# Two low-rank norms in a transformer block: row sums by transposing products and a small root, or sums over all partitions at once and a root on 128x512

## The chip, the cores and the metric

The kernel runs on one core of a Trainium2 chip. The metric is device time in microseconds (us) of one execution, the median of several. Each engine takes its own instructions in order and waits on semaphores: TensorE (PE; its weight loads are listed as PEld), VectorE (DVE), ScalarE (ACT), GpSimd (POOL) and SyncE (SP), which issues most of the transfers.

## What is computed

One block on 512 tokens of width 1024: a projection of the normalised input, a gated linear attention (GLA, 4 heads), a latent attention (MLA, 8 heads), a merge, and a squared-ReLU MLP. The change concerns the two latents of the MLA branch: `cq` (384 features) and `ckv` (256 features) are normalised per token before they are multiplied up to queries, keys and values.

```python
def rmsnorm(x, g):
    xf = x.astype(jnp.float32)
    y = xf * lax.rsqrt(jnp.mean(xf * xf, axis=-1, keepdims=True) + EPS)
    return (y * g.astype(jnp.float32)).astype(x.dtype)
...
    n = rmsnorm(h, g_mix[l])
    proj = n @ w_in[l]
    (gq, gk, gv, gr, z_gf, z_gb, cq, ckv, kr, z_ma, z_mb) = jnp.split(proj, SPLIT_IDX, axis=-1)
...
    q = (rmsnorm(cq, g_q) @ w_uq).reshape(B, S, H, MLA_QK_HEAD)
    kv = (rmsnorm(ckv, g_kv) @ w_ukv).reshape(B, S, H, MLA_NOPE + MLA_V)
```

## The kernel before

Precision is kept by splitting each fp32 operand into a rounded half and a rest (`split`: ACT writes the rounded half, DVE the rest); a product is then three PE passes (`mm3`: half by half, half by rest, rest by half). A projection of 128 columns (`proj_run`) is 24 matmuls of 512 columns. The input's own norm is applied afterwards: `R` (128x512) holds each token's factor on every partition, `r_x` (128x4) the same factors with tokens on partitions.

The latents are kept transposed, features on partitions and tokens along the row. `Latent.keep` stores a 128-feature piece with its gain (`cqc0` to `cqc2`, `ckvc0`, `ckvc1`) and its squares; `add_squares` adds those up into one 128x512 tile (`cqs2`, `ckvs1`). What is left to sum is over partitions, and this is done in four steps:

- `sums` (with `feature_sums`): four fp32 matmuls per latent, whose weights are 128 tokens of the squares and whose moving operand is one column of ones. Their result (`cqss`, `ckvss`) is 128x4, tokens on partitions. Two small DVE operations make it a mean, and POOL takes the power -1/2 on 128x4 (`cqr`, `ckvr`).
- `diagonals`: DVE multiplies by `r_x`, splits the 128x4 result and writes two 128x512 tiles of diagonal blocks (`cqdg`, `ckvdg`).
- `spread`: two matmuls of 512 columns with the matrix of ones bring every token's factor to every partition (`cqrs`, `ckvrs`, in PSUM).
- `normed`: DVE multiplies the kept pieces by that, ACT writes rounded halves (`cqhl0` to `cqhl2`, `ckvhl0`, `ckvhl1`), DVE the rests.

The work around it: for each GLA head h, `gla_scores` (tiles `bd`, `sc0`, `sc1`, `kt`), the gates of head h+1 (tile `l`, by ACT's exponential and logarithm, sums by DVE scans), `gla_state` (`gla2st`), `gla_out` (`gla2o`, `gla3o`), the squares and the root of the head's output (`gla2ss`, on ACT and POOL), and `gla_turn`, transposes of a finished head (`y12` to `y15`). Projections of the merge gate (`zb4` to `zb7`) and of queries and keys (`gq3`, `gk3`) lie between. For head 3 come the products that use the normalised latents: `ro0`, `ro1` (rotary part of the queries, from `cqhl` and the weights `wr0`, `wr1`, whose rests POOL computes), `uq0`, `uk0`, `uv0x`.

The order on each engine is fixed. Up to the end of the loop over heads 0 to 2 it is the order of the code; from there on, instructions are held back and issued by a long list of names (`SEQUENCE`), one queue letter and tile for each (`P` PE, `A` ACT, `D` DVE, `G` POOL, `S` SP). Stages of weights share rings of few buffers, so a transfer waits for the last reader of the buffer that it takes. PSUM has two rings of four banks ("at" and "mm"). At the very end, 20 matmuls of 64 columns into an unused tile (`tail`) run on PE behind the last product, while the last rows are scaled and stored.

Of the kernel before, what the change touches and what calls it, by code (L numbers as in the profile page):

```python
# [97 lines left out]
def tile_block(ctx: ExitStack, tc: tile.TileContext, t, out: bass.AP):  # L98
# [198 lines left out]
    def feature_sums(sq, name, tag="at"):
        tot = ps(tag, f"{name}ss")
        for j in range(NT):
            nc.tensor.matmul(tot[:, j : j + 1], sq[:, j * P : (j + 1) * P], ones[:, 0:1], start=True, stop=True)  # L300
        return tot
# [1707 lines left out]
    for x in range(2):  # L2009
# [4 lines left out]
        S:wr1f P:ckvss*4 D:ckvr D:cqc1 P:kt*4 S:wr1f D:ckvr P:y15*4 A:cqhl1 G:ckvr A:bds P:sc1*5 A:cqhl2 D:sc0 P:y14*4
        D:zb4 A:wr0h A:wk0h D:ckvr D:cqhl2 G:wr0l A:wk0h A:qF D:sc1*2 D:cqhl0 A:sc1 S:wk1f D:ckvrh D:ckvdg D:krsin
        D:ckvrl D:ckvdg D:cqhl1 D:sc1 P:zb5*24 A:wr1h D:sc0 A:yg4 D:zb5 G:wr1l A:cos D:kswap A:yg5 G:wk0l S:wq0f
        P:ro0*9 A:kT D:kr P:ckvrs*2 S:wq0f A:wk1h A:wk0h G:wk1l S:wq0f A:sc0 D:roa1 G:qF A:wk0h D:roa0 D:kr P:ro1*9
        G:wk0l D:ckvc0 D:ckvc1 A:ckvhl0 D:ckvhl0 D:kT A:tb5 D:rob1 A:wk1h D:rob0 A:kbuf0 D:roa0 A:ckvhl1 D:kbuf0
        A:wq0h P:zb6*24 A:ro0 D:sc0 G:wq0l D:ro0 G:wk1l S:zb7f P:gla3st*12 A:gla3s D:ckvhl1 G:wk0l P:gla3o1*12 D:roa1
        G:wk0l D:gla3s A:ro1 P:gla3o0*12 D:zb6 S:wq1f D:ro1 S:wq1f S:kbuf1 P:uq0*9 S:q001 S:q000 P:gla3o0*6 A:gla3sq  # L2020
        S:wq1f A:wk1h P:gla3o1*6 A:zb7h S:q000 G:wk1l S:q001 A:gla3sq P:uk0*6 D:zb7l A:gla3sq S:q211 A:q000 S:q110
        A:kbuf0 S:wq2f P:uv01*12 A:kbuf1 D:kbuf0 S:q110 A:gla3sq A:v01 G:gla3ss S:kbuf2 G:gla3ss A:wq1h S:q011 A:wk1h
        G:gla3ss A:q010 G:wq1l S:q010 D:grc D:grb S:q010 D:kbuf1 S:wq2f D:q011 S:w2_10 D:q001 S:wk2f D:grb D:v01
        S:q011 P:zb7*24 D:zb7 S:q211 P:s00*3 D:grc S:q210 P:s01*3 S:w2_20 D:top01 S:w2_30 D:top00 S:wq2f A:e00 P:uq1*9
        A:tb4 P:y17*4 A:q100 P:y16*4 A:e01 P:s03*3 S:q110 D:top03 A:wk2h S:q111 P:s11*3 A:yg6 G:wk2l D:tot00 D:e01
        S:kbuf3 A:e00 G:wk1l D:top11 A:e03 S:q111 P:uk1*6 D:q101 S:bo11f A:kbuf2 P:s02*3 A:wq2h S:q111 A:e11 P:s10*3
        G:wq2l S:bo11f D:top10 S:w2_20 D:top02 A:e10 A:e02 P:uv11*12 P:tp000*4 P:tp001*4 A:wk2h D:tot02 D:kbuf2
        A:pT000 G:wk2l D:tot10 A:tb6 S:kbuf3 D:pT010 P:uv10*12 S:w2_00 A:v10 P:s12*3 A:e02 S:q100 D:top12 A:pT001
        S:q100 D:e03 A:bo11h S:wk3f D:v10 P:uv00*12 S:q101 A:yg7 P:s13*3 P:uq2 D:top13 A:v00 S:kbuf2 A:e10 D:e11
        S:q101 D:pT011 A:e13 D:v00 A:e12 P:uq2*8 D:bo11l A:wk2h P:s31*3 G:wk2l A:tb7 P:tp010*4 P:tp011*4 A:pT000  # L2030
        D:top31 S:wq3f A:wk3h P:tp100*4 D:pT010 A:q200 S:wq3f A:e31 D:q201 D:tot12 P:uk2*6 D:e13 A:kbuf0 P:tp101*4
        S:q301 A:pT001 P:s21*3 S:h3 A:wk2h D:pT011 A:e12 G:wk2l D:top21 A:pT101 S:bo10f A:pT100 D:pT111 S:bo10f A:e21
# [15 lines left out]
        A:e50 P:s71*3 A:ghyo0 D:e61 G:w2_21 D:top71 A:e63 P:av4*4 G:w2_20 D:bo50l A:e71 P:s70*3 P:tp500*4 A:pT500
        D:tot62 P:tp510*4 S:w2_00 A:v30 D:top70 P:tp600*4 S:h2 A:gao1 D:e63 A:pT500 S:h0 D:pT510 G:gao1 A:pT600 S:h1
        D:v30 P:av4*7 D:pT510 G:yo1 P:wox0*3 D:tb4 P:tp501*4 G:zo0 A:pT501 P:wox1*3 G:glyo0 A:e70 D:pT511 P:s72*3  # L2050
        P:av5 D:pT610 P:tp511*4 G:my2 D:top72 A:pT501 P:s73*3 D:tot70 G:mx2 A:ghyo1 D:pT511 P:av5*2 A:e62 G:zo2 D:e71
# [149 lines left out]
```

## Time and profile before

| | |
|---|---|
| median of 3 runs | 732.03 us (731.73 to 732.14) |
| the profiled execution: its own time | 732.09 us |
| its span, first to last instruction | 730.3 us |
| around the span | 1.79 us |
| granted TensorE clock | 0.999 |
| busy: PE, DVE, ACT, POOL | 726.3, 619.8, 498.7, 225.8 us |

The page gives each engine's busy time and share of the span, the chain of work that ended last, and groups of instructions. The timeline gives start and duration of single instructions (neighbours merged, with their number), and in brackets how long the engine had been idle and for whom it waited. A line L90 or L76 is that of a recording helper, so instructions are told by their tiles.

### The profile page before, as it was taken

How to read it: one execution, taken by the hardware profiler on the slowest of the kernel's cores; microseconds unless marked ns; L12 is line 12 of the kernel's file. 1: busy time of each engine (PE TensorE's matmuls, PEld its weight loads, DVE VectorE, ACT ScalarE, POOL GpSimd, SP SyncE). 2: the span in 40 equal slices, each digit the busy share in tenths (PEclk: the TensorE clock that was granted, in tenths of full speed). 3: DMA queues.
4: the chain of work that ended last, by engine and by line, in shares of the span. 5: the costliest groups of instructions: out<-in, count | busy, mean ns of one | idle time of the engine just before them, and what ended most of it. 6: DMA issues, size and time to landing. Idle time of an engine off the chain costs nothing.

```text
span 730.3 us, 11455 instructions
## 1 busy us (share of the span) xinstructions
PE 726.3 (99%) x4174; PEld 641.2 (88%) x4174; DVE 619.8 (85%) x859; ACT 498.7 (68%) x846; POOL 225.8 (31%) x290
## 2 busy tenths in 40 slices
PE   9999999999999999999999999999999999999998
PEld 8888888888888888888888999889988998899987
DVE  6677887889988897789999789998699869987797
ACT  7456565595696864988866889545774477646976
POOL 1842020243843843226763512200111012100224
PEclk9999999999999999999999999999999999999999
DMA  9968683521222324657957899871987088814864
GB/s 323 346 176 198 210 180 88 84 62 29 58 58 59 89 46 110 184 158 189 251 88 208 196 205 201 187 215 57 245 182 201 9 223 206 206 59 134 183 89 143
DMA packets 82777, 112.06 MB, mean 153 GB/s; under 512 B 16384, under 2 KB 35712, under 8 KB 82720
## 3 DMA queue, kind: packets, MB, share of 16 engines
q1 hardware_dynamic: 65344, 77.81, 34.0%
q0 software_dynamic: 17088, 33.30, 27.3%
q8 instruction: 33, 0.54, 0.3%
q10 hardware_dynamic: 288, 0.22, 0.1%
q14 instruction: 24, 0.20, 0.1%
HBM read 106.32 MB, written 2.10 MB: 148 GB/s over the span
## 4 chain that ended last, share of the span: by engine, by line
PE 99%; issue 0%
PE f3x L90 3%; PE f2x L90 3%; PE f1x L90 3%; PE f0x L90 3%; PE first L90 3%; PE s L76 3%; PE av L76 3%; PE wox L76 3%; PE g2x L90 3%; PE g1x L90 3%; PE g0x L90 3%; PE gvx L90 3%; PE zax L90 3%; PE grx L90 3%; PE gk L90 2%; PE cq L90 2%
## 5 line engine op out<-in xcount | busy, mean ns | idle before, releaser
L90 POOL DMA_DIRECT2D w<-in_w_ff x32 | 38.6, 1205 | 240.1 <-DMA w<-in_w_ff 134.8
L76 ACT ACTIVATE e<-s,top 128x512 f32<-128x512 f32 x32 | 21.9, 688 | 8.5 <-DVE top L76 7.4
L76 DVE TENSOR_REDUCE top<-s 128x1 f32<-128x512 f32 x32 | 21.6, 682 | 5.8 <-PE s L76 5.6
L76 PE MATMUL s<-kbuf,q 96*128 96x512 f32 x96 | 26.3, 400 | 0.0
L76 PE MATMUL av<-pT,v 128*128 128x512 f32 (+1 forms) x108 | 25.2, 371 | 0.0
L76 DVE TENSOR_TENSOR pT<-tp,pT 128x512 fp32r<-128x512 f32 x32 | 21.7, 683 | 2.4 <-ACT pT L76 1.0
L76 ACT ACTIVATE pT<-tp 128x512 fp32r<-128x512 f32 x32 | 18.5, 596 | 6.1 <-PE tp L76 5.9
L76 PEld LDWEIGHTS av<-pT,v 128*128 128x128 f32 x108 | 18.6, 188 | 3.3
L76 PEld LDWEIGHTS s<-kbuf,q 96*128 96x128 f32 x96 | 17.2, 189 | 3.3 <-DVE grb L76 0.2
L76 PE MATMUL tp<-ident,e 128*128 128x128 f32 x128 | 17.1, 272 | 0.0
L76 PEld LDWEIGHTS tp<-ident,e 128*128 128x128 f32 x128 | 15.0, 141 | 2.2 <-ACT e L76 0.2
L90 POOL DMA_DIRECT2D gvw<-in_w_in x4 | 4.8, 1226 | 38.7 <-DVE gvw L90 34.0
L90 POOL TENSOR_TENSOR qF<-qk,qF 128x512 fp32r<-128x512 f32 x3 | 5.3, 1761 | 32.8 <-ACT qF L90 32.8
L90 POOL DMA_DIRECT2D zaw<-in_w_in x4 | 4.8, 1216 | 32.4 <-DVE zaw L90 27.7
L76 POOL DMA_DIRECT2D w<-in_w_ff x8 | 10.0, 1354 | 15.1 <-DVE g360l L76 7.1
L90 DVE TENSOR_TENSOR w<-w,w 128x1024 f32<-128x1024 f32 x12 | 14.4, 1220 | 0.1
L90 ACT ACT_TABLE_LOAD x9 | 11.5, 1283 | 1.2 <-PEq L2171 0.8
L76 POOL DMA_DIRECT2D w<-in_w_out x10 | 12.2, 1452 | 0.0
L76 ACT ACTIVATE e<-e,tot 128x512 f32<-128x512 f32 x16 | 11.3, 720 | 0.0
L76 POOL TENSOR_TENSOR my<-tb,yg 128x256 f32<-128x256 f32 x8 | 6.2, 772 | 15.6 <-DVE tb L76 9.4
L90 ACT ACTIVATE f1h<-f1a 128x512 fp32r<-128x512 f32 x10 | 6.1, 621 | 6.2 <-DVE f1a L90 6.2
L90 ACT ACTIVATE f2h<-f2a 128x512 fp32r<-128x512 f32 x10 | 6.1, 620 | 6.2 <-DVE f2a L90 6.2
(1975 smaller groups left out, 3099.7 us busy)
## 6 DMA issues: line engine op xcount, KB each, us to landing
w<-in_w_ff SPq DMA_DIRECT2D x48, 512.0 KB, 5.7
w<-in_w_ff POOLq DMA_DIRECT2D x40, 512.0 KB, 6.2
w<-in_w_out POOLq DMA_DIRECT2D x10, 512.0 KB, 6.1
grw<-in_w_in SPq DMA_DIRECT2D x8, 512.0 KB, 9.0
...
```

The lines of the kernel that those rows point to most:

```text
L76: what(*args, **options)
L90: return what(*args, **options)
```

## The change

The small root and the spreading go. The squares are split into rounded half and rest (`halves`, tile `cqq` or `ckvq`), and two matmuls of 512 columns with the matrix of ones sum them over the features and give the sums to every partition at once (`sums`, tile `cqss` or `ckvss`, now 128x512). DVE and POOL multiply the mean by `R` twice (`cqt`, `ckvt`). The root is taken on 128x512: ACT logarithm (`log`, `cqy`), ACT exponential of -1/2 of it and ACT square (`root`, `cqw`), then a Newton step (`refined`): one multiplication by `R` (on DVE for `cq`, on POOL for `ckv`) and two scalar_tensor_tensor operations on DVE. `normed` multiplies by this tile from SBUF, not by one in PSUM.

```diff
-        def sums(self):
-            tot = feature_sums(self.sqs[-1], self.name)
-            self.r = r = sm(f"{self.name}r")
-            nc.vector.scalar_tensor_tensor(r, tot[:, 0:NT], 1.0 / (self.n * P), r_x2, op0=ALU.mult, op1=ALU.mult)
-            nc.vector.tensor_scalar(r, r, EPS, None, op0=ALU.add)
-            nc.gpsimd.tensor_tensor(r, r, mhalf.to_broadcast([P, NT]), op=ALU.pow)
-        def diagonals(self):
-            nc.vector.tensor_tensor(self.r, self.r, r_x, op=ALU.mult)
-            self.diag = rounded_diagonal(self.r, self.name)
-        def spread(self):
-            self.rs = spread(self.diag, self.name, "mm")
+        def halves(self):
+            self.parts = u4(f"{self.name}q")
+            split(self.parts[:, 0, :], self.parts[:, 1, :], self.sqs[-1])
+        def sums(self, tag):
+            tot = ps(tag, f"{self.name}ss")
+            for x in range(2):
+                nc.tensor.matmul(tot, ones_r, self.parts[:, x, :], start=x == 0, stop=x == 1)
+            self.mean = m = u2(f"{self.name}t")
+            nc.vector.scalar_tensor_tensor(m, tot, 1.0 / (self.n * P), R, op0=ALU.mult, op1=ALU.mult)
+            nc.gpsimd.tensor_tensor(m, m, R, op=ALU.mult)
+        def log(self):
+            self.y = u2(f"{self.name}y")
+            nc.scalar.activation(self.y, self.mean, AF.Ln, bias=eps[:, 0:1])
+        def root(self):
+            self.w = w = u4(f"{self.name}w", F32)
+            nc.scalar.activation(self.y, self.y, AF.Exp, scale=-0.5)
+            nc.scalar.activation(w[:, 0], self.y, AF.Square)
+        def refined(self, by):
+            w = self.w
+            by.tensor_tensor(w[:, 1], self.y, R, op=ALU.mult)
+            nc.vector.scalar_tensor_tensor(w[:, 0], self.mean, EPS, w[:, 0], op0=ALU.add, op1=ALU.mult)
+            nc.vector.scalar_tensor_tensor(w[:, 0], w[:, 0], -3.0, w[:, 1], op0=ALU.add, op1=ALU.mult)
...
-                nc.vector.tensor_tensor(c, c, self.rs, op=ALU.mult)
+                nc.vector.scalar_tensor_tensor(c, c, -0.5, self.w[:, 0], op0=ALU.mult, op1=ALU.mult)
...
-        for _ in range(20):
+        for _ in range(36):
             nc.tensor.matmul(tail[:, : P // 2], ones_r, ones_r[:, : P // 2], start=True, stop=True)
...
     SEQUENCE = """
-        S:w2_11 S:zb6f S:w2_01 S:wr0f*2 A:sin A:zb6h D:cqc2 S:wk0f D:zb6l S:wr0f P:bd*4 D:cqc0 S:wr1f P:sc0*5 A:cqhl0
+        S:w2_11 S:zb6f S:w2_01 S:wr0f*3 D:cqw*3 A:ckvq D:ckvq A:zb6h A:sin A:cos D:cqc0 D:zb5l P:bd*4 P:sc0*5 A:cqhl0
```

The calls move with it. In the loop, the sums of `cq` come behind `gk3` instead of ahead of it; its logarithm stands at head 2 beside the gates' logarithm, its exponential behind `ckv1`; the transposes `y12`, `y13` and their copies go behind `gla2o`; the Newton step of `cq` and the split of `ckv`'s squares stand at the start of the listed part, ahead of the rest of `zb5`'s weights. There, sine and cosine come together, and a logarithm and an exponential of `ckv` follow. The tail is 36 matmuls instead of 20.

The order on PE at the first sums, before and after. `gq`, `gk` are the projections of head 3, `bd` the first tile of head 2's scores.

```order
L90 MATMUL gq_379_1983<-xT_8_89,gq3h_1980 128x512 x2
L90 MATMUL gq_379_1983<-xT_8_89,gq3l_1981 128x512
L90 MATMUL cqss_2185<-ones,cqs_389_2027 128x1 x4
L90 MATMUL gk_403_2078<-xT_1_82,gk3h_2074 128x512 x2
L90 MATMUL gk_403_2078<-xT_1_82,gk3l_2075 128x512
```

```order
L90 MATMUL gk_403_2078<-xT_8_89,gk3h_2074 128x512 x2
L90 MATMUL gk_403_2078<-xT_8_89,gk3l_2075 128x512
L90 MATMUL cqss_2214<-cqq_2178,ones_r 128x512 x2
L90 MATMUL bd_2220<-qkb_1938 128x128 x4
L90 MATMUL sc_424_2225<-qk_412_2132,qk_411_2131 128x256 x3
```

The four narrow products stood ahead of `gk`; the two wide ones stand behind it.

The order on DVE from the addition of `ckv`'s squares on, before and after. `zb5l`, `zb6l` are rests of weights, `cqc_119` is piece 0 of `cq`, `cqc_331` piece 1, `cqc_388` piece 2, `sc_488` (before) and `sc_487` (after) a tile of head 3's scores.

```order
L90 TENSOR_TENSOR ckvs_482_2504<-ckvs_482_2504,ckvs_455_2351 128x512
L90 TENSOR_TENSOR zb5l_2510<-zb5f_2507,zb5h_2509 128x1024
L76 TENSOR_TENSOR zb6l_2570<-zb6f_2568,zb6h_2569 128x1024
L76 TENSOR_TENSOR cqc_119_623<-cqc_119_623,cqrs_2475 128x512
L76 SCALAR_TENSOR_TENSOR ckvr_2548<-ckvss_2547,r_x_80 128x4
L76 TENSOR_TENSOR cqc_331_1728<-cqc_331_1728,cqrs_2475 128x512
L76 TENSOR_SCALAR ckvr_2548<-ckvr_2548 128x4
L76 COPY_PREDICATED sc_488_2539<-after,bds_2542 128x128
```

```order
L90 TENSOR_TENSOR ckvs_480_2495<-ckvs_480_2495,ckvs_454_2345 128x512
L76 TENSOR_TENSOR cqw_2497<-cqy_2331,R 128x512
L76 SCALAR_TENSOR_TENSOR cqw_2497<-cqt_2217,cqw_2497 128x512
L76 SCALAR_TENSOR_TENSOR cqw_2497<-cqw_2497 128x512
L76 TENSOR_TENSOR ckvq_2540<-ckvs_480_2495,ckvq_2540 128x512
L76 SCALAR_TENSOR_TENSOR cqc_119_623<-cqc_119_623,cqw_2497 128x512
L76 TENSOR_TENSOR zb5l_2504<-zb5f_2501,zb5h_2503 128x1024
L76 SCALAR_TENSOR_TENSOR ckvt_2542<-ckvss_2541,R 128x512
L76 SCALAR_TENSOR_TENSOR cqc_331_1728<-cqc_331_1728,cqw_2497 128x512
L76 TENSOR_TENSOR zb6l_2562<-zb6f_2560,zb6h_2561 128x1024
L76 SCALAR_TENSOR_TENSOR cqc_388_2025<-cqc_388_2025,cqw_2497 128x512
L76 COPY_PREDICATED sc_487_2532<-after,bds_2535 128x128
```

Four operations stand between the addition and `cqc0`, the rests of `zb5` and `zb6` move behind them, and the multiplications by the norm read two SBUF tiles.

The order on POOL from the latent `ckv` on, before and after (`wr0l` to `wk1l` are rests of weights, `qF` a rest of scaled queries).

```order
L76 TENSOR_TENSOR ckvr_2548<-ckvr_2548,mhalf 128x4
L76 TENSOR_TENSOR wr0l_2564<-wr0f_2562,wr0h_2563 128x384
L76 TENSOR_TENSOR wr1l_2567<-wr1f_2565,wr1h_2566 128x384
L76 TENSOR_TENSOR wk0l_2599<-wk0f_2597,wk0h_2598 128x128
L76 TENSOR_TENSOR wk1l_2629<-wk1f_2627,wk1h_2628 128x128
```

```order
L76 TENSOR_TENSOR ckvt_2542<-ckvt_2542,R 128x512
L76 TENSOR_TENSOR wr0l_2556<-wr0f_2554,wr0h_2555 128x384
L76 TENSOR_TENSOR wr1l_2559<-wr1f_2557,wr1h_2558 128x384
L76 TENSOR_TENSOR ckvw_2581<-ckvy_2550,R 128x512
L76 TENSOR_TENSOR wk0l_2591<-wk0f_2589,wk0h_2590 128x128
L76 TENSOR_TENSOR wk1l_2621<-wk1f_2619,wk1h_2620 128x128
```

A power on 128x4 has become a multiplication on 128x512, and a second multiplication on 128x512 stands behind `wr1l`.

More of the change, by code (lines that the diff above doesn't have):

```diff
@@ L291, in proj_T @@
         return proj_run(proj_begin(w_in, col, name, tag), xT)
-    r_x, r_x2 = one([P, NT], F32, "r_x"), one([P, NT], F32, "r_x2")
+    r_x, eps = one([P, NT], F32, "r_x"), one([P, NT], F32, "eps")
     R = one([P, S], F32, "R")
[L297 to L301, printed above, removed]
     def rounded_diagonal(r, name):
@@ L499, in tile_block @@
         lows()
-    nc.gpsimd.tensor_tensor(r_x2, r_x, r_x, op=ALU.mult)
+    nc.gpsimd.memset(eps, EPS)
     nc.scalar.activation(R, spread(x_diag, "x"), AF.Copy)
@@ L1405, in tile_block @@
             ckv_.begun[1], lows = begin_late(C_CKV + P, "ckv1")
-        (rotary.angles, rotary.reduced, cq_.diagonals)[h]()
+        if h < 2:
+            (rotary.angles, rotary.reduced)[h]()
         gate.sums("f")
@@ L1409, in tile_block @@
         state = gla_state(h, keys)
+        if h == 2:
+            cq_.log()
         gate.exps("f")
@@ L1418, in tile_block @@
             latent.add_squares()
-        if h:
-            gla_turn(h - 1)
+        if h == 1:
+            gla_turn(0)
         if h < 2:
@@ L1427, in tile_block @@
             scaled_qk.split_pairs()
+        else:
+            zb = begin(C_ZB + 4 * P, "zb4")
+            gla_turn(1)
         scaled_qk.across("b", gate.parts)
@@ L1434, in tile_block @@
             else:
+                cq_.halves()
                 ckv_.begin(0)
-                cq_.sums()
             finish_qk(h + 2, 1, w_k)
+            if h:
+                cq_.sums("at")
         else:
-            zb = begin(C_ZB + 4 * P, "zb4")
             scaled_qk.split_pairs()
             gla_gated(h, os, rs)
-            cq_.spread()
             ckv_.keep(1, ckv_.products(1))
+            cq_.root()
             ckv_.add_squares()
-            w_b = begin(C_ZB + 5 * P, "zb5")
+            w_b, lows = begin_late(C_ZB + 5 * P, "zb5")
             zb = proj_run(zb, xT)
@@ L1455, in tile_block @@
     far = far_queries(far)
-    ckv_.sums()
+    lows()
+    cq_.refined(nc.vector)
+    ckv_.halves()
+    ckv_.sums("mm")
     zb5 = proj_run(w_b, xT)
@@ L1460, in tile_block @@
     late = [over_rms(acc, f"b{f}") for f, acc in ((4, zb), (5, zb5))]
-    ckv_.diagonals()
+    ckv_.log()
     state = gla_state(h, keys)
@@ L1470, in tile_block @@
     rs = gla_squares(h, os)
-    ckv_.spread()
+    ckv_.root()
+    ckv_.refined(nc.gpsimd)
     ckv = ckv_.normed()
@@ L2012, in tile_block @@
     SEQUENCE = """
-        S:w2_11 S:zb6f S:w2_01 S:wr0f*2 A:sin A:zb6h D:cqc2 S:wk0f D:zb6l S:wr0f P:bd*4 D:cqc0 S:wr1f P:sc0*5 A:cqhl0
[L2014 to L2032, printed above, removed]
@@ L2048, in tile_block @@
[L2048 to L2051, printed above, removed]
-        P:tp601*4 A:pT601 G:glyo1 D:v31 A:e72 D:top73 A:e70 P:av5*9 D:pT611 A:e73 P:wox0 P:tp610*4 D:tot72 A:pT600
@@ L2053, in tile_block @@
-        D:tb5 P:tp700*4 A:pT700 P:tp701*4 D:pT610 G:my2 P:tp611*4 D:pT710 A:pT601 G:yo2 P:wox1*3 A:e72 D:pT611 G:mx2
+        S:w2_11 S:zb6f S:w2_01 S:wr0f*3 D:cqw*3 A:ckvq D:ckvq A:zb6h A:sin A:cos D:cqc0 D:zb5l P:bd*4 P:sc0*5 A:cqhl0
+        S:wr1f*3 P:ckvss*2 D:ckvt D:cqc1 G:ckvt D:zb6l S:wk0f A:cqhl1 D:cqc2 P:kt*4 P:y15*4 A:bds A:wr0h A:yg5 P:sc1*5
+        D:sc0 P:y14*4 A:cqhl2 A:yg4 D:zb4 D:cqhl0 G:wr0l D:cqhl1 D:sc1*2 A:ckvy D:cqhl2 S:wk1f D:krsin P:zb5*24 A:wr1h
+        A:sc1 D:sc1 A:ckvy A:ckvw A:wk0h*2 G:wr1l A:qF G:ckvw D:sc0 D:zb5 D:kswap G:wk0l S:wq0f P:ro0*9 A:kT D:kr
@@ new lines, in tile_block @@
+        D:ckvw*2 S:wq0f A:wk1h A:wk0h G:wk1l S:wq0f A:sc0 D:roa1 G:qF A:wk0h D:roa0 D:kr P:ro1*9 G:wk0l D:kT D:ckvc0
+        D:ckvc1 A:ckvhl0 D:ckvhl0 A:tb5 D:rob1 A:wk1h D:rob0 D:sc0 A:kbuf0 D:roa0 A:ckvhl1 D:kbuf0 A:wq0h P:zb6*24
+        A:ro0 G:wq0l D:ro0 G:wk1l S:zb7f P:gla3st*12 A:gla3s D:ckvhl1 G:wk0l P:gla3o1*12 D:gla3s G:wk0l D:roa1 A:ro1
+        P:gla3o0*12 D:zb6 S:wq1f D:ro1 S:wq1f S:kbuf1 P:uq0*9 S:q001 S:q000 P:gla3o0*6 A:gla3sq S:wq1f A:wk1h
+        P:gla3o1*6 A:zb7h S:q000 G:wk1l S:q001 A:gla3sq P:uk0*6 D:zb7l A:gla3sq S:q211 A:q000 S:q110 A:kbuf0 S:wq2f
@@ new lines, in tile_block @@
+        P:uv01*12 A:kbuf1 D:kbuf0 S:q110 A:gla3sq A:v01 G:gla3ss S:kbuf2 G:gla3ss A:wq1h S:q011 A:wk1h G:gla3ss A:q010
+        G:wq1l S:q010 D:grc D:grb S:q010 D:kbuf1 S:wq2f D:q011 S:w2_10 D:q001 S:wk2f D:grb D:v01 S:q011 P:zb7*24 D:zb7
+        S:q211 P:s00*3 D:grc S:q210 P:s01*3 S:w2_20 D:top01 S:w2_30 D:top00 S:wq2f A:e00 P:uq1*9 A:tb4 P:y17*4 A:q100
+        P:y16*4 A:e01 P:s03*3 S:q110 D:top03 A:wk2h S:q111 P:s11*3 A:yg6 G:wk2l D:tot00 D:e01 S:kbuf3 A:e00 G:wk1l
+        D:top11 A:e03 S:q111 P:uk1*6 D:q101 S:bo11f A:kbuf2 P:s02*3 A:wq2h S:q111 A:e11 P:s10*3 G:wq2l S:bo11f D:top10
@@ new lines, in tile_block @@
+        A:pT200 P:tp210*4 D:pT211 G:mx0 A:wk3h P:s53*3 A:e30 D:tot32 D:pT210 G:my0 A:pT200 D:top53 G:w2_00 D:pT210
+        P:uv21*12 A:wq3h P:tp211*4 D:e31 A:e53 P:s52*3 P:av2 A:pT201 D:top52 A:gao0 P:s43*3 D:top43 A:e52 G:gao0
+        P:s40*3 D:pT211 A:v20 D:top40 A:e43 P:av2*5 G:wk3l D:tot52 D:v11 G:wq3l A:e40 D:e33 P:s42*3 A:e32 G:wk3l
+        S:bo21f A:e52 D:e53 P:s41*3 P:uq3 S:w2_30 G:wk3l P:tp300*4 P:tp301*4 D:top41 S:q310 A:pT301 D:v20 S:bo21f
+        A:e41 P:av2*5 D:top42 S:w2_01 A:v21 S:q311 A:pT300 D:v21 S:w2_21 D:pT310 P:uq3*8 S:w2_11 A:q300 D:tot40
@@ L2077, in tile_block @@
         G:ms2 P:g3x1*3 A:gend D:ms0 S:out*2 A:ms1 S:out*2 D:h3 G:ms3 A:junk P:g3x0*12 S:out G:hp3 D:h2 D:hend A:junk
-        P:g3x1*12 A:hp2 D:h3 D:hp2 A:junk A:ms2 S:out D:ms2 S:out D:ms3 D:hp3 P:gend*14 P:tail*20 A:junk D:ms3 A:hp3
+        P:g3x1*12 A:hp2 D:h3 D:hp2 A:junk A:ms2 S:out D:ms2 S:out D:ms3 D:hp3 P:gend*14 P:tail*36 A:junk D:ms3 A:hp3
         D:hp3 D:ms3 A:ms3 S:out A:out
```

37 lines of the change are left out of this document (22 added, 15 removed).

## The prediction

> **What bounds the kernel now.** I read the page first, then the chain, then PE's waits, then the timeline of the stretch in which the latents are normalised.
>
> ```profile
> PE 726.3 (99%) x4174; PEld 641.2 (88%) x4174; DVE 619.8 (85%) x859; ACT 498.7 (68%) x846; POOL 225.8 (31%) x290
> ...
> PE 99%; issue 0%
> ```
>
> PE is busy for the whole span, and the chain that ended last is PE alone. What PE no longer does is won, and each wait that the change puts on PE is lost; nothing later takes it up. The chain gives the price of what leaves (start, duration, tile, count of passes):
>
> ```profile
> 162.22 5.44 PE gk L90 x24
> ...
> 219.78 0.79 PE cqss L90 x8
> 220.56 5.61 PE gk L90 x24
> ...
> 241.66 0.46 PE cqrs L90 x2
> ...
> 254.73 0.79 PE ckvss L76 x8
> ...
> 265.28 0.47 PE ckvrs L76 x2
> ```
>
> The second question is how much room the other engines have. The table of windows gives busy time from 249 to 279 us, and the list of waits the one that PE's weight loads show there:
>
> ```profile
> 249.00:279.00 30.00, 30.00 (x171) 26.10 (x170) 27.66 (x46) 18.21 (x32) 15.75 (x18) 1.00 0.33 64
> ```
>
> ```profile
> PEld ro L76 <- DVE cqhl L76: 0.2, 1, 0.2
> ```
>
> DVE (third pair of numbers) is busy for 27.7 of 30 us, and PE already waits for it, for the rests of `cqhl`. So here PE bounds the time and DVE follows closely. That is where the change adds DVE work.
>
> **The change part by part.** *PE.* Four pieces leave: 0.79 + 0.46 + 0.79 + 0.47 = 2.51 us. The `gk` behind the narrow products takes 5.61 where another takes 5.44, so 0.17 more. Two pairs of 512-column products come, each like `cqrs`: 0.92. Net: 2.51 + 0.17 - 0.92 = 1.76 us less. The transposes `y12`, `y13` only change place.
>
> *The tail.* Sixteen more matmuls at 2.31 / 20 = 0.12 us make it end at 724.85 + 36 x 0.12 = 729.1.
>
> ```profile
> 724.85 2.31 PE L76 MATMUL tail<-ones_r 128*128 128x64 f32 x20
> ...
> 726.79 0.35 ACTq L76 DMA_DIRECT2D out<-ms  x1
> ```
>
> ```profile
> DMA to landing us min/median/max: 1.8/2.3/4.1
> ```
>
> The last store lands at about 726.8 + 2.3 = 729.1 and hides it: cost 0, and 0.3 at most if PE ends last.
>
> *How DVE and POOL share.* The change gives POOL three multiplications on 128x512 from two SBUF tiles (`cqt`, `ckvt`, `ckvw`), and DVE many operations with two SBUF inputs, so the price of their meeting is needed:
>
> ```profile
> 191.12 3.67 POOL L90 TENSOR_TENSOR qk<-qkf,c3f 128x256 f32<-128x256 f32 x3
> ...
> 244.38 1.75 POOL L90 TENSOR_TENSOR qk<-qkf,c3f 128x256 f32<-128x256 f32 x3
> ```
>
> ```profile
> 193.21 1.10 DVE L90 TENSOR_TENSOR qkb<-gkn,eeb 128x512 f32<-128x512 f32 x1
> ...
> 242.10 0.68 DVE L90 TENSOR_TENSOR qkf<-gkn,eef 128x512 f32<-128x512 f32 x1
> 242.71 0.68 DVE L90 TENSOR_TENSOR qkb<-gqn,eeb 128x512 f32<-128x512 f32 x1
> ```
>
> Three POOL operations take 1.75 us alone and 3.67 beside DVE; a DVE operation takes 0.68 alone (one every 0.61 in a row) and 1.10 beside them. They take turns: each waits until the other's instruction is over. A DVE operation caught by a POOL multiplication on 128x512 (1.29 alone) thus loses up to 1.1 us:
>
> ```profile
> 267.05 1.29 POOL L76 TENSOR_TENSOR qF<-qk,qF 128x512 fp32r<-128x512 f32 x1
> ```
>
> These are TENSOR_TENSORs. For a SCALAR_TENSOR_TENSOR with both tiles in SBUF, as the new ones are, there is one meeting: it takes 0.90 with POOL in its way until 718.33, and 0.75 alone.
>
> ```profile
> 717.99 0.90 DVE L76 SCALAR_TENSOR_TENSOR ms<-h,hp,gfin 128x512 f32<-128x512 f32 x1
> ...
> 724.08 0.75 DVE L76 SCALAR_TENSOR_TENSOR ms<-h,hp,gfin 128x512 f32<-128x512 f32 x1
> ```
>
> ```profile
> 716.70 1.63 POOL L76 TENSOR_TENSOR ms<-h,gfin 128x512 f32<-128x512 f32 x1
> ```
>
> I take it to wait alike. Were it free, 1.7 us of the waits below would go (rival A). The Trainium skill ("SBUF — State Buffer", section "Who interferes with whom") says that a VectorE instruction with two SBUF inputs is blocked for the whole of a GpSimd instruction that reads SBUF, and makes no exception for one with a scalar; by that the sum stands as it is.
>
> *Where DVE starts.* At head 2 the first `gla2` row waits for POOL's root:
>
> ```profile
> 246.50 2.06 POOL L90 TENSOR_TENSOR gla2ss<-gla2ss,mhalf 128x4 f32<-128x4 f32 x1
> ...
> 285.25 1.01 POOL L76 TENSOR_TENSOR gla3ss<-gla3ss,mhalf 128x4 f32<-128x4 f32 x1
> ```
>
> ```profile
> 246.45 1.23 DVE L90 TENSOR_TENSOR zb4l<-zb4f,zb4h 128x1024 fp32r<-128x1024 f32 x1 [1.87 <-ACT zb4h L90]
> ...
> 248.87 0.88 DVE L90 SCALAR_TENSOR_TENSOR grb<-gla2o,gla2ss,grb 128x256 f32<-128x256 f32 x2 [0.19 <-POOL gla2ss L90]
> ...
> 250.44 0.68 DVE L90 TENSOR_TENSOR ckvs<-ckvs,ckvs 128x512 f32<-128x512 f32 x1
> 251.04 1.63 DVE L90 TENSOR_TENSOR zb5l<-zb5f,zb5h 128x1024 fp32r<-128x1024 f32 x1
> ...
> 255.56 0.16 DVE L76 SCALAR_TENSOR_TENSOR ckvr<-ckvss,r_x 128x4 f32<-128x4 f32 x1 [0.73 <-PE ckvss L76]
> ...
> 257.50 0.30 DVE L76 COPY_PREDICATED sc<-after,bds 128x128 f32<-128x128 int32 x1 [1.11 <-ACT bds L76]
> ...
> 270.92 0.68 DVE L76 TENSOR_TENSOR kT<-kt,kT 128x512 fp32r<-128x512 f32 x1
> ...
> 274.27 0.69 DVE L76 TENSOR_TENSOR sc<-sc,sc 128x512 fp32r<-128x512 f32 x1
> ```
>
> The root loses 1.05 us to `zb4l` today (2.06 against 1.01). In the new order `zb4l` comes sooner, among POOL's products ahead of that root, and POOL's `cqt` meets DVE's masking of the scores earlier on. I take 0.5 us later for `grb` (between 0 and 1.1): 249.4. `zb4l` itself then costs PE 0.1.
>
> *First wait: `ckvss`.* `ckvs` starts 1.57 behind `grb`, at 250.95, followed by three `cqw` and the rest `ckvq`: four steps of 0.61, 0.1 because the third needs the second, and 0.8 for two turns of POOL (`zb5l`, in that place today, loses 0.4 to one: 1.63 against 1.23). `ckvq` is done at 250.95 + 0.61 + 3 x 0.61 + 0.1 + 0.8 + 0.68 = 255.0. PE is 0.96 us early there (1.76 less 0.47 for `ckvrs`, less the rest of the second pair: 0.33), less 0.1:
>
> ```profile
> 254.57 0.95 PE L76 MATMUL ckvss<-ones,ckvs 128*128 128x1 f32 x8
> ...
> 265.59 0.64 PE L76 MATMUL ro<-cqhl,wr1h 128*128 128x512 f32 x2
> ...
> 274.55 3.04 PE L76 MATMUL gla3o<-gv,sc 128*128 128x256 f32 x24
> ```
>
> Its second product could start at 254.57 - 0.86 + 0.23 = 253.94. Wait: 1.1. `cqc0`, `zb5l` (1.14: `zb4l`'s 1.23 less the overlap of 0.08), `ckvt` follow and are done at 257.3, just when PE comes to `zb5`: 0.
>
> *Second and third wait: `ro0`, `ro1`.* Two more prices, of DVE's masking and of a rest of weights on POOL:
>
> ```profile
> 227.97 1.37 DVE L90 COPY_PREDICATED sc<-after,bds 128x128 f32<-128x128 int32 x4 [1.07 <-PE sc L90]
> ```
>
> ```profile
> 263.63 1.06 POOL L76 TENSOR_TENSOR wr1l<-wr1f,wr1h 128x384 fp32r<-128x384 f32 x1 [3.70 <-ACT wr1h L76]
> ```
>
> DVE goes on with `cqc1`; POOL's `ckvt` then holds `zb6l` back by 1.1, and POOL's `wr0l` holds `cqc2` back by 0.85: 261.65. One masking (0.34), `zb4`, two rests, two maskings (0.66) and the rest of `cqhl2` end at 265.0; PE, now only 0.15 ahead of today, wants it for the last but one product of `ro0`: at 265.59 (today's `ro1`) - 0.47 (`ckvrs`) - 0.46 - 0.15 = 264.5. Wait: 0.5. On ACT, `cqhl2` (behind `cqc2`), a copy, a table load, the logarithm and `wr1h` take 0.6 + 0.6 + 1.28 + 0.6 + 0.5, so `wr1h` is there at 265.2 and POOL's `wr1l` 1.1 later, at 266.3; PE's third product of `ro1` could start at 264.5 + 0.5 + 0.46 + 0.46 = 265.9. Wait, with the signal: 0.5. PE is then 0.35 behind today: -0.15 - 0.47 + 0.5 + 0.5 = 0.38.
>
> The load is taken from its row, where the next operation starts when it ends:
>
> ```profile
> 232.78 1.28 ACT L90 ACT_TABLE_LOAD   x1
> 234.08 1.06 ACT L90 ACTIVATE l<-l 128x1024 f32<-128x1024 f32 x1
> ```
>
> The Trainium skill ("ScalarE: Activation LUTs", section "What ACT_TABLE_LOAD costs") adds about 1.38 us of draining to every switch, 2.66 in all; these rows show none, and by that figure `wr1h` would come 1.4 later and the sum would be over 1 us larger.
>
> *Fourth and fifth wait: `kT`, `sc0`.* From ACT's `sc1` (0.6 behind `wr1h`: 265.8) to `kT`, DVE has eleven operations, 7.0 us by their steps today, and 1.6 for turns of POOL (1.1 at `ckvw`, 0.5 at two small ones): 274.4. PE wants it for the third pass of `gla3st`, whose twelve passes of 0.12 precede `gla3o`: 274.55 - 1.43 + 0.24 + 0.35 = 273.7. Wait: 0.7. Six steps later `sc0` is done at 274.3 + 6 x 0.61 = 278.0. Today it ends at 274.96, and PE wants it 1.68 behind the start of `gla3o` (half of its passes and two), at 276.23; with PE 1.05 behind today, at 277.3. Wait: 0.7. Behind `sc0` DVE only has what the next products do not need at once.
>
> *Sum.* Waits 0.1 + 1.1 + 0.5 + 0.5 + 0.7 + 0.7 = 3.6; products -1.8; tail 0. Against the profiled execution's 732.09 (span 730.3 and 1.8 around it; 0.06 above the median): 732.09 + 1.8 = 733.9. The crude account agrees: eight DVE steps more (4.9) against about 2.4 for two diagonals and small ones, 1.8 of idle time filled (0.73 and 1.11), a later start, and some 2.5 more in turns.
>
> **The rivals.** *A: it comes out even.* The turns cost half: POOL's products fall beside DVE operations that read PSUM (`zb4`, `roa`), or only TENSOR_TENSORs wait (then a `cqw` saves 0.4, `cqc2` 0.85, the `ckvw` steps 0.45). The waits shrink by 1.7, to 1.9: 732.2. For it: the one meeting of a SCALAR_TENSOR_TENSOR shows only 0.15 of delay, and my times are good to half a microsecond each. Against: `cqc1`, `zb6l`, `cqc2` stand in a row where `ckvt` and `wr0l` fall, and none reads PSUM.
>
> *B: faster.* DVE keeps ahead. Without turns and with `grb` at 248.87, `ckvq` is done at 253.7, ahead of PE's 253.9, and `sc0` near 273, over 1 us before PE wants it. The full 1.76 is won: 730.3. It decides as soon as the turns and the later start cost under about 1.5 us together. Against: the turns in the rows above.
>
> *C: loads twice as long.* If each table load kept ACT as long again (1.28), `wr1l` would come 1.3 later and PE with it, and the exponential behind a second load 2.6 later, half of it hidden since DVE is late itself: 733.9 + 1.3 = 735.2. The rows of the load show the next operation at once. The figure of the Trainium skill's page on ScalarE, above, would give this case.
>
> *D: the products do not get cheaper* because the wide pair waits for weights: `cqrs` has the same form, and 0.46 leaves no room. I give it nothing of its own.
>
> **How the numbers follow.** A measurement of this kernel tells 0.2% (1.5 us) from no change. My forecast, with C (0.02) and what comes out over 733.5, has 0.45; A, between 730.6 and 733.5, 0.40; B, when nearly all is won, 0.15. The likeliest case alone runs from 733.5 to 735.1. The range goes from 730.9, which leaves out most of B, to 735.1, where the collisions and the start (1.1) cost their upper bounds.
>
> **What would show it.** Right: PE's waits name DVE `ckvq` at the second product of `ckvss` (about 1 us), DVE `cqhl` and POOL `wr1l` at `ro`, DVE `kT` and `sc` behind; `zb6l` takes over 2 us. Wrong: no wait of PE between 250 and 280 (then B); waits of 2 us or less in all (A); a chain that ends in something other than PE; or waits outside this stretch, which I do not expect.

## The result: 736.99 us, slower by 0.67%, and the profile after

The changed kernel takes 736.99 us (median of 6 runs, 736.29 to 737.34), the kernel before 732.05 (6 runs, 731.68 to 732.57). The ratio is 1.0067, 95% interval 1.0054 to 1.0080. Forecast were 733.9 and at most 735.1: the direction came as expected, the loss is 4.9 us instead of 1.8. The profiled execution is the fastest of the six, 736.29 with a span of 734.6, so the trace has to explain 4.2 us.

The page of the changed kernel, busy time and then the chain that ended last:

```profile
PE 728.4 (99%) x4174; PEld 640.4 (87%) x4174; DVE 626.4 (85%) x854; ACT 504.0 (69%) x855; POOL 226.9 (31%) x291
...
PE 81%; DVE 10%; DMA 3%; ACT 2%; POOL 2%; issue 1%; SPq 1%; DVEq 0%; ACTq 0%; POOLq 0%
```

The share of PE (TensorE) says nothing, 99% as before: the longer tail adds busy time that is no work. The chain says it: PE alone before, now a tenth of it is DVE (VectorE). Links of it in order of time (start, duration, engine, tile):

```profile
250.36 0.78 DVE grc L90 x2
251.15 0.60 DVE ckvs L90
251.74 2.05 DVE cqw L76 x2
...
281.64 0.87 DVE ckvhl L76
282.51 0.61 DVE gla3s L76
283.12 0.04 issue
283.16 1.58 PE gla3o L76 x11
```

The chain is in DVE's queue from the gated rows at 250 to `gla3s` at 283, and only there does it go back to PE. One longer passage of it, from 261.8 to 265.9, is on ACT: `cqhl2`, a copy, the table load, the logarithm, `wr1h` and the copy `sc`, for which DVE stands 0.56 us. The same 30 us as in the window of before (PE, PEld, DVE, ACT, POOL):

```profile
249.00:279.00 30.00, 27.75 (x148) 22.73 (x147) 28.56 (x41) 21.28 (x36) 14.10 (x19) 1.00 0.26 46
```

PE is down from 30.00 to 27.75, DVE up from 27.66 to 28.56. The list of PE's waits (total, times, longest), where before there was none in this stretch:

```profile
PE gla3o L76 <- DVE gla3s L76: 1.0, 1, 1.0
...
PE ckvss L76 <- DVE ckvq L76: 0.7, 1, 0.7
PE gla3o L76 <- DVE sc L76: 0.7, 1, 0.7
PE gla3st L76 <- DVE kT L76: 0.6, 1, 0.6
PE ro L76 <- POOL wr1l L76: 0.3, 1, 0.3
```

The last four are waits of the forecast, which had walked through them as `ckvq`, `wr1l`, `kT`, `sc0`; the one that it had for the rests of `cqhl` shows only in the weight loads (PEld, 0.4). The first and longest of the list is not in the forecast. The list gives only the time in which PE stood idle. For what a place costs one reads where PE's products start, before and after. First before, then after:

```profile
214.15 0.63 PE L90 MATMUL gq<-xT,gq3h 128*128 128x512 f32 x2
...
277.43 0.63 PE L76 MATMUL uq<-cqhl,wq0h 128*128 128x512 f32 x2
...
280.93 0.63 PE L76 MATMUL uk<-ckvhl,wk0h 128*128 128x512 f32 x2
```

```profile
214.25 0.63 PE L90 MATMUL gq<-xT,gq3h 128*128 128x512 f32 x2
...
279.81 0.63 PE L76 MATMUL uq<-cqhl,wq0h 128*128 128x512 f32 x2
...
283.16 1.58 PE L76 MATMUL gla3o<-gla3s,qF 128*128 128x256 f32 x11 [1.01 <-DVE gla3s L76]
284.58 0.63 PE L76 MATMUL uk<-ckvhl,wk0h 128*128 128x512 f32 x2
...
728.63 4.10 PE L76 MATMUL tail<-ones_r 128*128 128x64 f32 x36
```

The first transfers put the executions up to 1.7 us apart, so every place is counted from the first product of `gq3` (214.15 before, 214.25 after), which lies ahead of everything the change touches. From there the changed kernel's PE is, against before:

| place | forecast | measured |
|---|---|---|
| start of `zb4` (247.41; after 246.66) | -0.96 | -0.85 |
| `kt`, behind `ckvss` (255.38; 255.51) | -0.15 | +0.03 |
| `zb6`, behind `ro1` (267.68; 268.28) | +0.4 | +0.50 |
| `uq0`, behind `sc0` (277.43; 279.81) | +1.8 | +2.28 |
| `uk0`, behind `gla3s` (280.93; 284.58) | +1.8 | +3.55 |
| start of the tail (724.85; 728.63) | +1.8 | +3.68 |
| end of the span (730.3; 734.6) | +1.8 | +4.2 |

So the forecast holds to half a microsecond until `uq0`; 1.3 us come in one step at `gla3s`, 0.1 behind it and 0.5 from the tail's start to the end of the span.

### The profile page after: what moved, and what is told of

It reads as the page before. It is cut to its first block, busy times and chain, and to the rows that moved or that the text cites. A ratio compares the mean times of both kernels' runs of the same rounds, so it can differ in the third digit from the quotient of the medians.

```text
span 734.6 us, 11464 instructions
## 1 busy us (share of the span) xinstructions
PE 728.4 (99%) x4174; PEld 640.4 (87%) x4174; DVE 626.4 (85%) x854; ACT 504.0 (69%) x855; POOL 226.9 (31%) x291
## 4 chain that ended last, share of the span: by engine, by line
PE 81%; DVE 10%; DMA 3%; ACT 2%; POOL 2%; issue 1%; SPq 1%; DVEq 0%; ACTq 0%; POOLq 0%
PE f3x L90 3%; PE f2x L90 3%; PE f1x L90 3%; PE f0x L90 3%; PE s L76 3%; PE av L76 3%; PE wox L76 3%; PE g2x L90 3%; PE g1x L90 3%; PE g0x L90 3%; PE gvx L90 3%; PE zax L90 3%; PE grx L90 3%; PE g3x L76 2%; PE tp L76 2%; PE f3z L90 2%
## 5 line engine op out<-in xcount | busy, mean ns | idle before, releaser
L90 POOL TENSOR_TENSOR qk<-qkf,c3f 128x256 f32<-128x256 f32 x11 | 10.8, 1008 | 0.2
```

Source lines behind the costliest of these rows:

```text
L90: return what(*args, **options)
```

## The experiments

Theory 1: DVE's queue between 249 and 284 us sets the time, made longer by the new steps and by its turns with POOL (GpSimd); what PE loses is DVE's lateness at the end of that queue. In the changed kernel DVE itself waits for nothing from PE in this stretch. Its rivals: each wait is a loss of its own; POOL costs DVE nothing; the loss lies in the tail, in ACT's table loads or in the products. Each ratio is against the kernel before, timed beside it (medians 732.05 to 732.21). The last two columns are read from each profile: the tail's start, counted from `gq3`, and the start of DVE's last rest of `ro1` (279.01 before, 284.46 after), counted alike, both against before.

| kernel | median us | ratio to before, 95% interval | PE at the tail | DVE at `ro1` |
|---|---|---|---|---|
| changed | 736.99 | 1.0067 (1.0054 to 1.0080) | +3.68 | +5.35 |
| changed, once more (e9) | 736.66 | 1.0059 (1.0047 to 1.0072) | +3.69 | +5.33 |
| e1 tail of 20 | 736.38 | 1.0060 (1.0048 to 1.0073) | +3.74 | +5.36 |
| e2 state first | 736.40 | 1.0064 (1.0050 to 1.0078) | +3.84 | +5.48 |
| e3 products on DVE | 735.11 | 1.0041 (1.0029 to 1.0054) | +2.18 | +3.46 |
| e4 no Newton step | 733.87 | 1.0024 (1.0014 to 1.0033) | +0.85 | +2.44 |
| e5 `wr1h` first | 737.32 | 1.0070 (1.0056 to 1.0084) | +4.10 | +5.65 |
| e6 before, rests twice | 736.45 | 1.0060 (1.0047 to 1.0072) | +4.72 | +4.52 |
| e7 no root | 730.65 | 0.9981 (0.9972 to 0.9990) | -1.88 | -1.01 |
| e8 light | 732.13 | 0.9998 (0.9989 to 1.0006) | -0.90 | +0.73 |
| e11 light, state first | 732.09 | 0.9998 (0.9989 to 1.0007) | -0.63 | +0.97 |
| e10 before, tail of 36 | 732.14 | 1.0000 (0.9991 to 1.0009) | +0.04 | not changed |

**e1, the tail alone.**

```diff
-        for _ in range(36):
+        for _ in range(20):
```

> The changed kernel with 20 instead of 36 matmuls in the tail. Changed kernel 736.99, tail of 36 measured 3.94 us (0.11 each). Theory (the tail only shows where it outlives the last store): the tail then ends 1.75 us sooner, but the last store allows only 0.35 of that: about 736.6. Rival (the end of the kernel follows PE's last matmul): 735.2.

Measured: 736.38, with PE's way to the tail unchanged (+3.74). By the medians (736.99, or 736.66 in e9) it is 0.3 to 0.6 less, within the spread of the runs; 1.75 is ruled out.

**e2, the longest wait alone.**

```diff
-A:ro0 G:wq0l D:ro0 G:wk1l S:zb7f P:gla3st*12 A:gla3s D:ckvhl1 G:wk0l P:gla3o1*12 D:gla3s
+A:ro0 G:wq0l G:wk1l S:zb7f P:gla3st*12 A:gla3s D:gla3s D:ro0 D:ckvhl1 G:wk0l P:gla3o1*12
```

> The changed kernel with VectorE's combining of the state (gla3s) put ahead of the rests ro0 and ckvhl1. Theory (VectorE's queue up to gla3s places TensorE behind gla3o, and the 1.27 us that TensorE stands there is all lost): gla3s comes 1.8 us sooner, the wait goes, ro0 and ckvhl1 are still in time: 735.8. Rival (the next late rest takes the same wait): 737.0.

Measured: 736.40, which lies between the two numbers and does not decide. On PE's way nothing is won (+3.84 instead of +3.68), so the rival is right. PE's waits in this kernel, where `gla3s` is gone and two others have come:

```profile
PE zb L76 <- DVE zb7l L76: 0.5, 1, 0.5
PE s L76 <- DVE q L76: 0.4, 1, 0.4
```

DVE writes `roa1` at 283.09, when it did in the changed kernel (283.03); ACT has `ro1` next in its queue, waits for it, and holds the copies `zb7h`, `q` and `kbuf` behind it. The lateness is that of the queue's end; `gla3s` was only the first product to feel it. Theory 1 stays, my number for this run does not.

**e3, POOL's multiplications on DVE.**

```diff
-            nc.gpsimd.tensor_tensor(m, m, R, op=ALU.mult)
+            nc.vector.tensor_tensor(m, m, R, op=ALU.mult)
...
-    ckv_.refined(nc.gpsimd)
+    ckv_.refined(nc.vector)
```

In DVE's order the second step of `ckvt` stands behind `cqc1`, and that of `ckvw` ahead of the other two.

> The changed kernel with the three 128x512 multiplications of GpSimd (cqt, ckvt, ckvw) on VectorE. Theory (GpSimd's instruction holds a VectorE instruction of two SBUF inputs for its whole length): zb6l goes from 2.32 back to about 1.2 and kr from 1.78 to 0.7, which gives 2.2, and two more VectorE steps in the stretch cost 1.2: 1.0 less, 736.0. Rival (only the number of VectorE steps counts): 1.2 more, 738.2.

Measured: 735.11, PE 1.5 earlier: DVE does two steps more in the stretch and is 1.9 us sooner through. POOL in the changed kernel, then DVE beside it:

```profile
257.53 1.68 POOL L76 TENSOR_TENSOR ckvt<-ckvt,R 128x512 f32<-128x512 f32 x1 [4.29 <-DVE ckvt L76]
259.69 1.47 POOL L76 TENSOR_TENSOR wr0l<-wr0f,wr0h 128x384 fp32r<-128x384 f32 x1 [0.48 <-ACT wr0h L76]
...
267.91 1.35 POOL L76 TENSOR_TENSOR ckvw<-ckvy,R 128x512 f32<-128x512 f32 x1 [1.43 <-ACT ckvy L76]
```

```profile
252.69 1.10 DVE L76 SCALAR_TENSOR_TENSOR cqw<-cqt,cqw 128x512 f32<-128x512 f32 x1
253.82 0.69 DVE L76 SCALAR_TENSOR_TENSOR cqw<-cqw 128x512 f32<-128x512 f32 x1
...
257.97 2.32 DVE L76 TENSOR_TENSOR zb6l<-zb6f,zb6h 128x1024 fp32r<-128x1024 f32 x1
260.22 1.50 DVE L76 SCALAR_TENSOR_TENSOR cqc<-cqc,cqw 128x512 f32<-128x512 f32 x1
...
268.03 1.78 DVE L76 TENSOR_TENSOR kr<-kr,cos 32x512 f32<-32x512 f32 x1
```

And DVE in e3:

```profile
259.47 1.22 DVE L76 TENSOR_TENSOR zb6l<-zb6f,zb6h 128x1024 fp32r<-128x1024 f32 x1
260.61 0.68 DVE L76 SCALAR_TENSOR_TENSOR cqc<-cqc,cqw 128x512 f32<-128x512 f32 x1
...
267.61 0.68 DVE L76 TENSOR_TENSOR kr<-kr,cos 32x512 f32<-32x512 f32 x1
```

`zb6l` loses 1.10, `kr` 1.10, and `cqc2` 0.82 more that I had not counted for this run, since `wr0l` then meets other operations. The rival (only the number of steps counts) is out. `cqc2` and the second `cqw` are SCALAR_TENSOR_TENSORs: they wait as TENSOR_TENSORs do.

**e4, no Newton step.** The factor is then the exponential times R, without the correction; ACT's square, which only the Newton step reads, goes too.

```diff
-            nc.vector.scalar_tensor_tensor(w[:, 0], self.mean, EPS, w[:, 0], op0=ALU.add, op1=ALU.mult)
-            nc.vector.scalar_tensor_tensor(w[:, 0], w[:, 0], -3.0, w[:, 1], op0=ALU.add, op1=ALU.mult)
...
-                nc.vector.scalar_tensor_tensor(c, c, -0.5, self.w[:, 0], op0=ALU.mult, op1=ALU.mult)
+                nc.vector.scalar_tensor_tensor(c, c, 1.0, self.w[:, 1], op0=ALU.mult, op1=ALU.mult)
```

> The changed kernel without the Newton step: the factor is the exponential times R, so two VectorE scalar_tensor_tensor operations and one ScalarE square less for each latent. Theory (VectorE's queue between 249 and 283 sets the time): the two at cqw took 1.10 and 0.69 and the two at ckvw 0.84 and 0.76 with their turns, about 3.2 together; all of it is won: 733.8. Rival (the losses sit in ScalarE's table loads, in the products or in the tail): within 0.7 of 737.0.

Measured: 733.87. DVE is 2.9 sooner through, PE 2.8 sooner at the tail. Table loads, products and tail are as in the changed kernel, and DVE stands 0.56 us for ACT's `sc` as there, so the rival is out as the main cause. What these 0.56 us behind the table load cost was not tried alone.

**e5, one wait in the middle alone.**

```diff
-A:cqhl2 A:yg4
+A:cqhl2 A:wr1h A:yg4
...
-P:zb5*24 A:wr1h A:sc1
+P:zb5*24 A:sc1
```

> The changed kernel with ScalarE's copy wr1h put right behind cqhl2, ahead of the transposes' copy and the table load, so that GpSimd's wr1l is ready about 2 us sooner. Theory (VectorE's queue up to 284 us places TensorE; a wait ahead of its end is taken up by the next one): the wait for wr1l goes, the wait for kT grows by the same half microsecond, and the time stays within 0.3 of the changed kernel's 737.0. Rival (the waits of TensorE add up, each is lost by itself): 0.5 less, 736.5.

Measured: 737.32, PE 0.4 later. The wait for `wr1l` is gone and that for `kT` is 0.8 instead of 0.6, as theory 1 has it, and the rival's half microsecond is not won. But the move is not quite neutral: counted from `gq3`, `wr1l` came 2.6 us sooner on POOL, and there it met two rests of `cqhl` on DVE, which take 1.28 together in the changed kernel; PE now waits 0.6 for rests of `cqhl`. At the end of its queue DVE is 0.3 later. POOL, then DVE:

```profile
263.38 1.12 POOL L76 TENSOR_TENSOR wr1l<-wr1f,wr1h 128x384 fp32r<-128x384 f32 x1 [1.70 <-ACT wr1h L76]
```

```profile
262.95 2.10 DVE L76 TENSOR_TENSOR cqhl<-cqc,cqhl 128x512 fp32r<-128x512 f32 x2
```

**e6, more DVE work in the kernel before.**

```diff
-                nc.vector.tensor_tensor(hl[:, 1, :], c, raw(hl[:, 0, :]), op=ALU.subtract)
+                for _ in range(2):
+                    nc.vector.tensor_tensor(hl[:, 1, :], c, raw(hl[:, 0, :]), op=ALU.subtract)
```

> The kernel before, in which VectorE computes the five rests of the normalised latents (cqhl0 to cqhl2, ckvhl0, ckvhl1) twice; nothing else differs. Five steps of 0.6 make VectorE 3.0 later at the end of the stretch. Theory (VectorE's queue decides, and it had 1.8 to spare: in the changed kernel it was 5.5 later and TensorE 3.65): 1.2 more, 733.3. Rival 1 (VectorE's work is hidden in this stretch): 732.1. Rival 2 (it has nothing to spare): 735.1.

Measured: 736.45, 4.3 more, beyond each of the three. That DVE's work decides is shown without any of the change's products, table loads or multiplications. My size failed twice. The 1.8 us to spare is that at the end of the queue; at `cqhl2` there is none, as the 0.2 us wait of before had said, and three rests more made `cqhl2` 3.1 late there, counted from `gq3` (their own 1.8, the rest in POOL's turns). PE waits 2.90 us in one piece, and then its products take almost twice as long. PE, and the windows behind the wait (PE, PEld, DVE, ACT, POOL, granted clock):

```profile
266.61 0.50 PE L76 MATMUL ro<-cqhl,wr0h 128*128 128x512 f32 x1 [2.90 <-DVE cqhl L76]
266.94 0.39 PE L76 MATMUL ro<-cqhl,wr0l 128*128 128x512 f32 x1
267.17 1.02 PE L76 MATMUL ro<-cqhl,wr0h 128*128 128x512 f32 x2
```

```profile
266.60:267.20 0.60, 0.59 (x3) 0.51 (x4) 0.60 (x2) 0.00 (x0) 0.00 (x0) 1.00 0.35 66
267.20:270.50 3.30, 3.30 (x9) 2.60 (x8) 3.24 (x6) 1.30 (x4) 1.75 (x2) 0.50 0.00 0
270.50:275.00 4.50, 4.50 (x21) 3.65 (x20) 4.30 (x8) 2.84 (x4) 1.48 (x2) 0.99 0.00 0
```

The clock is at 0.50 for 3.3 us, which by estimate costs half of that, 1.65; with the wait that is 4.55 of the 4.72 that PE loses. In the changed kernel no wait is over 1.01 and the clock stays at 1.00, from 249 to 279 (the window above) and from 279 to 284 alike. The Trainium skill ("TensorE: Matmul & The Clock Gate", section "Why this matters for your kernels") warns of idle gaps over about 3 us; here 2.90 was enough.

**e7, no root.** Logarithm, exponential, square, Newton step and the second factor R are left out (`normed` multiplies by the mean), and the tail is of 20.

```diff
-                nc.vector.scalar_tensor_tensor(c, c, -0.5, self.w[:, 0], op0=ALU.mult, op1=ALU.mult)
+                nc.vector.scalar_tensor_tensor(c, c, -0.5, self.mean, op0=ALU.mult, op1=ALU.mult)
```

> The changed kernel with a tail of 20 and without the root: logarithm, exponential, square, Newton step and the second multiplication by R are left out, and the latents are multiplied by the mean instead (another output). The products with ones and the order of the rest stay. Theory (the products save 1.76 us on TensorE, and only the work of the root takes it back): 732.05 - 1.76 = 730.3. Rival (the wide products are no cheaper, or the moved instructions cost time): 732.0 or more.

Measured: 730.65, 1.5 less than before; on PE's way 1.88 is won, where the forecast had 1.76 for the products. They are cheaper, by about what the rows said, and no cost of the moved instructions shows. None of PE's waits lies between 225 and 285 us.

**e8, e11, everything light.** e4, e3, e5 and e1 together, and then e2 on top.

> All together: no Newton step, the multiplications by R on VectorE, wr1h early, tail of 20. Theory (TensorE's place is VectorE's lateness less 1.8, and not before TensorE's own saving): of 5.5 us of lateness 3.2 go with the Newton steps and 1.8 with GpSimd's turns, 0.5 is left, TensorE is 1.3 ahead: 730.8. By adding the single gains (3.1, 1.9, 0.6): 731.4. Rival (TensorE's saving is lost elsewhere): 732.0.

> The light version (no Newton step, multiplications by R on VectorE, wr1h early, tail of 20) with VectorE's gla3s ahead of ro0 and ckvhl1. Theory (the one wait that is left in the stretch, 0.5 for gla3s, is real): 731.6. Rival (as when the same was done to the changed kernel, the end of VectorE's queue stays and a later product waits instead): 732.1.

Measured: 732.13 and 732.09, no difference from before (732.14 and 732.13), so in time the rivals' numbers came, not the theory's. On PE's way e8 wins 0.90 and e11 0.63, and the spans (medians 730.0 and 730.1, before 730.4) show 0.3 to 0.4 of it; in four runs of e8 2.5 to 2.8 us instead of 1.7 lie around the span, and why is open. PE's only wait between 225 and 285 in e8, which e11 takes away and does not win:

```profile
PE gla3o L76 <- DVE gla3s L76: 0.5, 1, 0.5
```

In e11 it is `zb7l` (0.2) and `q` (0.4) instead, as in e2. No version that still takes the root is measurably faster than before.

**e9, e10, the tail from the other side.** The changed kernel unaltered, and the kernel before with `range(36)`.

> The changed kernel unaltered, to have its time beside the next two on the same chip: 736.4 to 737.3, the spread of its six runs; its waits and the start of its tail as in its first profile (728.6), shifted by what the first transfers differ.

> The kernel before with 36 matmuls in the tail. In the changed kernel's profile 5.97 us lie between the tail's start and the end of the span, with 20 matmuls 5.48 (before 5.45). Theory (the longer tail outlives the last store by half a microsecond): 0.5 more, 732.6. Rival 1 (hidden by the store, as the prediction had it): 732.1. Rival 2 (sixteen matmuls in full): 733.9.

Measured: 736.66, with the same way of PE as in the first profile to 0.01; and 732.14 against 732.13, interval plus or minus 0.66 us. The traces put the tail at 0.2 to 0.5: from its start to the end of the span lie 5.45 before, 5.68 in e10 (724.62 to 730.3), 5.97 in the changed kernel. The full 1.9 is ruled out, the half microsecond of my theory is not shown.

## Why the forecast was right in kind and wrong in size

*Products, -1.8: right.* e7 wins 1.88 on PE's way.

*DVE becomes the bound, and PE waits for `ckvq`, `wr1l`, `kT`, `sc0`: right.* Up to `uq0` the walk gave +1.8 and the trace +2.28; `sc0` was forecast to be done at 278.0 and is at 278.46 (278.36 counted from `gq3`). Read from the starts of the products (the way to the next place against before, with the 0.33 and 0.47 added that leave at `ckvss` and `ro`), `ckvss` costs 0.92, `ro` 0.96, `kT` 0.86 and `sc0` 0.90, where the forecast had 1.1, 1.0, 0.7 and 0.7; that the errors have both signs is part of the agreement.

*Turns with POOL: right,* and shown by e3. The forecast took it that SCALAR_TENSOR_TENSORs wait too; e3's `cqc2` (1.50 against 0.68) settles it. The Trainium skill ("SBUF — State Buffer", section "Who interferes with whom") says that a VectorE instruction with two SBUF inputs contends with a GpSimd instruction that reads SBUF, and exempts no kind of operation with two such inputs; these rows agree.

*"Behind `sc0` DVE only has what the next products do not need at once": this step failed.* DVE after, from `sc0` on, and what POOL does there; then before:

```profile
277.78 0.68 DVE L76 TENSOR_TENSOR sc<-sc,sc 128x512 fp32r<-128x512 f32 x1
278.38 0.68 DVE L76 TENSOR_TENSOR roa<-roa,rob 128x512 f32<-128x512 f32 x1
279.09 1.40 DVE L76 TENSOR_TENSOR kbuf<-kr,kbuf 32x512 fp32r<-32x512 f32 x1
280.52 1.12 DVE L76 TENSOR_TENSOR ro<-roa,ro 128x512 fp32r<-128x512 f32 x1
281.56 0.95 DVE L76 TENSOR_TENSOR ckvhl<-ckvc,ckvhl 128x512 fp32r<-128x512 f32 x1
282.43 0.68 DVE L76 TENSOR_TENSOR gla3s<-gla3st,gla3s 128x512 fp32r<-128x512 f32 x1
```

```profile
278.55 1.39 POOL L76 TENSOR_TENSOR wq0l<-wq0f,wq0h 128x384 fp32r<-128x384 f32 x1 [5.15 <-ACT wq0h L76]
```

```profile
272.83 0.69 DVE L76 TENSOR_TENSOR roa<-roa,rob 128x512 f32<-128x512 f32 x1
273.55 0.68 DVE L76 TENSOR_TENSOR kbuf<-kr,kbuf 32x512 fp32r<-32x512 f32 x1
...
277.81 0.68 DVE L76 TENSOR_TENSOR gla3s<-gla3st,gla3s 128x512 fp32r<-128x512 f32 x1
```

The change moves `sc0` ahead of `roa0` and `kbuf0`. I counted the move as a gain for `sc0` and forgot that the two come behind it, ahead of `gla3s`, where `kbuf0` moreover falls beside POOL's `wq0l` (1.40 instead of 0.68); only `roa1` goes the other way, behind `gla3s`. From the end of `sc0` to the end of `gla3s` it is 4.65 now (278.46 to 283.11), 3.53 before (274.96 to 278.49). With 3.53 `gla3s` would by estimate be done at 281.99, when PE comes to it; the forecast put this wait at nothing, and it costs 1.3. By e2 that is not the wait for `gla3s` alone: with it gone, `zb7l` and `q` come too late by about as much. The crude account in the forecast was short in the same way, 3.7 of lateness where the end of the queue shows 5.35: the eight new steps and the later start are as reckoned, but by rough addition of the rows the two diagonals and small steps that go made 1.9 instead of 2.4, 1.2 of idle time was filled instead of 1.8, and what is left for the turns is some 3.1 instead of 2.5.

*That the loss is the sum of PE's waits: right as bookkeeping, wrong as a cause.* The idle times in the list add up to only 3.3. By the starts of the products the four places above cost 3.64, `gla3s` 1.27, `zb4` 0.29 and what lies behind `uk0` 0.13, 5.33 in all; less 0.85 + 0.33 + 0.47 = 1.65 for the products this is the 3.68 at the tail. But e2, e5 and e11 take a wait away and win nothing. The table of the experiments has the better sum: DVE's lateness at `ro1` less 1.6 is PE's loss at the tail. It gives 1.67 in the changed kernel, 1.62 in e1, 1.64 in e2, 1.28 in e3, 1.59 in e4, 1.55 in e5, 1.63 in e8 and 1.60 in e11. The 1.6 is read off these kernels, not derived. The sum fails where PE is bound by itself (e7) and where a product in the middle waits long (e6).

*Rivals.* A (even) and B (faster) had the turns cost less; e3 rules that out. D (products no cheaper) is ruled out by e7. C (each table load twice as long) is ruled out by the rows of ACT, where the next operation follows the load at once:

```profile
262.97 1.28 ACT L76 ACT_TABLE_LOAD   x1
264.27 0.72 ACT L76 ACTIVATE ckvy<-ckvt,eps 128x512 f32<-128x512 f32 x1
```

*The range.* Its upper end took the known waits at their worst, but nothing for a wait that the walk had not reached. Of the 4.2 us in the profile, 1.8 was forecast, 0.5 are errors up to `uq0`, 1.4 come at `gla3s` and behind it, 0.5 at the tail. The tail was put at 0 with the last store landing 2.3 us after its issue; from that issue to the end of the span lie 3.5 us before (726.79 to 730.3) and 4.0 in the changed kernel (730.58 to 734.6), and whether the tail makes this difference is open, as e10 does not show it. The rest up to 4.9 is the spread between executions: a second set of runs gave 736.66.
